# Rotary embedding: a second buffer for VectorE's sin products, so that a pass needs no separate wait instruction on VectorE

**Chip, cores, metric.** One core of one Trainium2 chip. The metric is device time in microseconds (us), the median of several runs.

## The reference

```python
batch, seq, dim, num_heads = 16, 512, 1024, 16          # x is float32, cos and sin are [seq, 32]
x = x.reshape(batch, seq, num_heads, head_dim)          # head_dim 64
x1, x2 = x[..., :half_dim], x[..., half_dim:]
rotated = np.concatenate([x1 * cos - x2 * sin,
                          x1 * sin + x2 * cos], axis=-1)
```

33.55 MB are read and 33.55 MB written. Per element there are some three arithmetic operations.

## The kernel before

x is cut into 8 slabs of 128 partitions x 8192 elements (4 MB each). Five slabs fit at a time; each is loaded by SyncE's queue and stored from the same memory by ScalarE's queue. A slab is worked on in two passes of 128x4096. In each pass ScalarE casts to bf16, VectorE makes a sin product (`t2`), a cos product in place and an add in place, and ScalarE converts back to f32.

```python
slabs  = ctx.enter_context(tc.tile_pool(name="slabs", bufs=slots))     # slots = 5
tpool  = ctx.enter_context(tc.tile_pool(name="tpool", bufs=3))         # xb, bf16
t2pool = ctx.enter_context(tc.tile_pool(name="t2pool", bufs=1))        # the sin products
# ... loads, tables ...
for i, u in enumerate(passes):
    if i + 1 < len(passes):
        cast(passes[i + 1])                       # ScalarE: xb <- slab
    s, k = u
    xs, xu = slab[s], xb.pop(u)
    t2 = t2pool.tile([P, PW], bf16, tag="t2")
    for t, a in ((t2, rpp * hd), (xu, 0)):        # sin product, then cos product in place
        nc.vector.tensor_mul(
            out=t, in0=xu,
            in1=view(tab, a + k * rows * hd, (hd, rows), (0, nh), (1, hd)))
    nc.vector.tensor_add(
        out=xu, in0=xu,
        in1=view(t2, half, (hd, rows * nh), (-half, 2), (1, half)))
    nc.scalar.copy(out=view(xs, k * PW, (1, PW)), in_=xu)              # back to f32
    if k == rpp // rows - 1:
        nc.scalar.dma_start(out=dram(out_flat, s), in_=xs)             # store
        if s + slots < nslabs:
            load(s + slots)
```

A framework orders the instructions of each engine and puts in the waits. With one `t2` buffer, the sin product of a pass must wait for the add of the pass before (which reads `t2`) as well as for ScalarE's cast. An instruction here carries one wait; the second becomes an instruction of its own ahead of it.

## Time and profile before

| | before |
|---|---|
| time, median of 3 | 162.83 us (162.74 to 163.21) |
| span of the profiled run | 160.8 us |
| VectorE busy, ScalarE busy | 111.7 us (69%), 114.8 us (71%) |
| moved by DMA | 67.25 MB, 418 GB/s over the span |

In the table of instruction groups a line gives the source line, the engine and operation, output and input, the count; then busy time and mean ns of one; then the idle time of the engine just ahead of them and what ended it. These are ScalarE's two conversions and VectorE's sin product, before:

```profile
L117 ACT CAST xb<-slab 128x4096 bf16<-128x4096 f32 x16 | 57.5, 3601 | 24.8 <-DMA slab<-in_x_dram 24.8
L137 ACT CAST slab<-xb 128x4096 f32<-128x4096 bf16 x16 | 57.7, 3604 | 7.2 <-DVE xb L133 7.1
L130 DVE TENSOR_TENSOR t<-xb,tab 128x4096 bf16<-128x4096 bf16 x16 | 36.7, 2292 | 19.4 <-ACT xb L117 18.6
```

Read from the last line upwards: VectorE's idle time is ended by ScalarE, and most of ScalarE's by DMA. The separate wait instructions stand in the view of VectorE's source line, as entries of its queue (minimum, median and maximum ns, then first and last start):

```profile
L130 DVEq EVENT_SEMAPHORE  x16: 21/21/21, 13.3 to 136.8; - x16
```

### The profile page before, as it was taken

To read this page: it belongs to the slowest core of one execution; us is meant where nothing else is said; L and a number is where in the kernel's file an instruction comes from. 1 tells how busy PE (TensorE), PEld (TensorE's weight loads), DVE (VectorE), ACT (ScalarE), POOL (GpSimd) and SP (SyncE) were. 2 spreads that over 40 slices of the span, in tenths; PEclk is the share of its full clock that TensorE was granted. 3 is DMA by queue.
4 is the path that set the end of the run, shared out by engine and by line. 5 is a ranking of instruction groups with operands and counts; after the bars stand their busy time and mean duration, and the time that the engine had idled before them with its cause. 6 is when DMAs were issued, how large, how long until landed. Compare 5 with 4: busy or idle time off the path is not lost.

```text
span 160.8 us, 197 instructions
## 1 busy us (share of the span) xinstructions
PE 0.6 (0%) x4; PEld 0.4 (0%) x4; DVE 111.7 (69%) x52; ACT 114.8 (71%) x33; POOL 2.3 (1%) x9
## 2 busy tenths in 40 slices
PE   0010000000000000000000000000000000000000
PEld 0000000000000000000000000000000000000000
DVE  0012799999999999999997599907997079970000
ACT  3007919999999999999994999069990699926000
POOL 5000000000000000000000000000000000000000
DMA  7999999999999999999999999999999999999993
GB/s 261 408 408 416 497 391 391 505 408 367 416 391 473 440 391 456 457 391 424 489 391 424 489 391 399 514 391 391 522 391 393 489 416 399 481 424 399 481 424 139
DMA packets 2369, 67.25 MB, mean 418 GB/s; under 512 B 288, under 2 KB 288, under 8 KB 320
## 3 DMA queue, kind: packets, MB, share of 16 engines
q1 hardware_dynamic: 1152, 33.55, 49.3%
q10 hardware_dynamic: 1152, 33.55, 48.3%
q0 software_dynamic: 64, 0.13, 0.2%
q14 instruction: 1, 0.01, 0.0%
HBM read 33.69 MB, written 33.55 MB: 418 GB/s over the span
## 4 chain that ended last, share of the span: by engine, by line
DMA 47%; ACT 22%; DVE 21%; issue 0%; ACTq 0%; SPq 0%; DVEq 0%
DMA slab<-in_x_dram 26%; DMA out_dram<-slab 21%; ACT slab L137 11%; ACT xb L117 11%; DVE xb L133 7%; DVE t L130 7%; DVE xb L130 7%; ACTq L137 0%; SPq L65 0%; DVEq L130 0%
## 5 line engine op out<-in xcount | busy, mean ns | idle before, releaser
L117 ACT CAST xb<-slab 128x4096 bf16<-128x4096 f32 x16 | 57.5, 3601 | 24.8 <-DMA slab<-in_x_dram 24.8
L137 ACT CAST slab<-xb 128x4096 f32<-128x4096 bf16 x16 | 57.7, 3604 | 7.2 <-DVE xb L133 7.1
L130 DVE TENSOR_TENSOR t<-xb,tab 128x4096 bf16<-128x4096 bf16 x16 | 36.7, 2292 | 19.4 <-ACT xb L117 18.6
L133 DVE TENSOR_TENSOR xb<-xb,t 128x4096 bf16<-128x4096 bf16 x16 | 36.7, 2292 | 0.5
L130 DVE TENSOR_TENSOR xb<-xb,tab 128x4096 bf16<-128x4096 bf16 x16 | 36.7, 2292 | 0.5
L92 DVE CAST tab<-raw 128x256 bf16<-128x256 f32 x1 | 0.3, 295 | 10.9 <-DMA raw<-in_sin_dram 10.9
L117 ACT ACT_TABLE_LOAD x1 | 1.3, 1283 | 0.7 <-PEq L158 0.7
L102 DVE CAST tab<-acc 128x512 bf16<-128x512 f32 x1 | 0.7, 692 | 0.7 <-PE acc L96 0.7
L75 POOL DMA_DIRECT2D raw<-in_cos_dram x1 | 0.7, 674 | 0.8 <-POOLq L158 0.8
L96 PE MATMUL acc<-tab,pick 128*128 128x128 bf16 x4 | 0.6, 302 | 11.2 <-DVE tab L92 11.2
L87 POOL TENSOR_SCALAR_AFFINE_SELECT pick<-pick 128x128 bf16<-128x128 bf16 x2 | 0.5, 288 | 0.1
L75 POOL DMA_DIRECT2D raw<-in_sin_dram x1 | 0.5, 534 | 0.0
L96 PEld LDWEIGHTS <-pick 128*128 128x128 bf16 x4 | 0.4, 128 | 11.1 <-issue 8.0
L104 DVE CAST tab<-acc 128x256 bf16<-128x256 f32 x1 | 0.4, 414 | 0.0
L106 DVE TENSOR_SCALAR tab<-acc 128x256 bf16<-128x256 f32 x1 | 0.4, 412 | 0.0
L84 POOL MEMSET pick<- 128x256 bf16 x1 | 0.3, 330 | 0.0
L158 POOL MEMSET const-float32-0.0<- 128x1 f32 x1 | 0.1, 99 | 0.2 <-issue 0.2
L158 POOL MEMSET const-uint8-127<- 128x1 uint8 x1 | 0.1, 102 | 0.0
L158 POOL MEMSET const-bfloat16-1.0<- 128x1 bf16 x1 | 0.1, 101 | 0.0
L158 POOL MEMSET const-float32-1.0<- 128x1 f32 x1 | 0.1, 98 | 0.0
## 6 DMA issues: line engine op xcount, KB each, us to landing
slab<-in_x_dram SPq DMA_DIRECT2D x8, 4096.0 KB, 28.2
out_dram<-slab ACTq DMA_DIRECT2D x8, 4096.0 KB, 28.4
raw<-in_cos_dram POOLq DMA_DIRECT2D x1, 64.0 KB, 6.9
raw<-in_sin_dram POOLq DMA_DIRECT2D x1, 64.0 KB, 8.9
```

The source lines that it names most:

```text
L75: nc.gpsimd.dma_start(out=view(raw, i * TR * half, (1, TR * half)), in_=bass.AP(tensor=src.tensor, offset=src.offset, ap=[[TR * half, P], ...
L84: nc.gpsimd.memset(pick, 0.0)
L87: nc.gpsimd.affine_select(out=part, in_=part, compare_op=mybir.AluOpType.not_equal, fill=1.0, base=-g, pattern=[[0, P // SP], [-G, SP]], c ...
L96: nc.tensor.matmul(view(acc, i * TW + g * TR * half, (1, TR * half)), view(pick, g * P, (1, P)), view(tab1, i * TR * half, (1, TR * half)) ...
L102: nc.vector.tensor_copy(out=view(tab, 0, (hd, 2 * rpp), (1, half)), in_=view(acc, 0, (half, 2 * rpp), (1, half)))
L104: nc.vector.tensor_copy(out=view(tab, half, (hd, rpp), (1, half)), in_=view(acc, 0, (half, rpp), (1, half)))
L106: nc.vector.tensor_scalar_mul(out=view(tab, rpp * hd + half, (hd, rpp), (1, half)), in0=view(acc, TW, (half, rpp), (1, half)), scalar1=-1.0)
L117: nc.scalar.copy(out=xb[u], in_=view(slab[s], k * PW, (1, PW)))
L130: nc.vector.tensor_mul(out=t, in0=xu, in1=view(tab, a + k * rows * hd, (hd, rows), (0, nh), (1, hd)))
L133: nc.vector.tensor_add(out=xu, in0=xu, in1=view(t2, half, (hd, rows * nh), (-half, 2), (1, half)))
L137: nc.scalar.copy(out=view(xs, k * PW, (1, PW)), in_=xu)
L158: nc = _bacc.Bacc("TRN2", target_bir_lowering=False, num_devices=1)
```

## The change

It is meant to let the sin product of a pass begin without asking whether the previous add has ended, so that VectorE has one wait, in the instruction itself, and no instruction for the other.

```diff
-    t2pool = ctx.enter_context(tc.tile_pool(name="t2pool", bufs=1))
+    t2pool = ctx.enter_context(tc.tile_pool(name="t2pool", bufs=2))
```

## The prediction

> **What bounds the kernel now.** I read four views: busy shares of the engines, the table by stage, the groups with what ended their idle time, then the tail in order of time. The page comes first.
>
> ```profile
> PE 0.6 (0%) x4; PEld 0.4 (0%) x4; DVE 111.7 (69%) x52; ACT 114.8 (71%) x33; POOL 2.3 (1%) x9
> DVE  0012799999999999999997599907997079970000
> ACT  3007919999999999999994999069990699926000
> DMA  7999999999999999999999999999999999999993
> DMA 47%; ACT 22%; DVE 21%; issue 0%; ACTq 0%; SPq 0%; DVEq 0%
> ```
>
> No compute engine is busy over 71% of the span, and both ScalarE and VectorE show holes late in it. The row that has none is DMA: 9 in every slice but the first and the last. The chain of waits gives VectorE 21%, which looks like room for a gain; the table by stage says why that is not to be believed. Its columns are: stretch, its length, PE, PEld, DVE, ACT, POOL busy, clock, DMA share, GB/s.
>
> ```profile
> 13.20:34.60 21.40, 0.00 (x0) 0.00 (x0) 17.27 (x9) 17.79 (x6) 0.00 (x0) 1.00 1.02 439
> 34.60:62.97 28.37, 0.00 (x0) 0.00 (x0) 27.60 (x13) 28.32 (x9) 0.00 (x0) 1.00 0.97 408
> 62.97:97.50 34.53, 0.00 (x0) 0.00 (x0) 30.97 (x15) 31.98 (x10) 0.00 (x0) 1.00 1.02 440
> 97.50:126.10 28.60, 0.00 (x0) 0.00 (x0) 20.44 (x9) 17.57 (x5) 0.00 (x0) 1.00 1.00 433
> 126.10:147.50 21.40, 0.00 (x0) 0.00 (x0) 13.75 (x6) 17.82 (x5) 0.00 (x0) 1.00 0.99 426
> 147.50:158.20 10.70, 0.00 (x0) 0.00 (x0) 0.00 (x0) 0.00 (x0) 0.00 (x0) 1.00 1.01 438
> ```
>
> Stage length times DMA share, summed, is 21.8 + 27.5 + 35.2 + 28.6 + 21.2 + 10.8 = 145.1 us of the 145.0 us from 13.2 to 158.2: the 16 DMA engines never lack work, whatever VectorE and ScalarE do (27.60 us of VectorE in one stage, 13.75 in another). The time is thus the 67.25 MB that the page counts (418 GB/s over the span), the start and the last store's completion.
>
> **What the Trainium skill says, and whether the trace agrees.** "Perfetto Trace Analysis", Identifying Dependency Chains: an instruction that waits on more than one engine may get an EventSemaphore instruction ahead of it for the further condition. The trace agrees: VectorE's queue holds 16 EVENT_SEMAPHORE of 21 ns, one ahead of each sin product, which waits both for ScalarE's cast of its input and for VectorE's own last read of the only sin buffer. "VectorE: DVE Perf Modes", The DRAIN you can't avoid: the next operation does not start before the pipe is empty, and a semaphore after each operation cost nothing extra in its measurement. The trace agrees for a wait inside an instruction (starts 2.32 to 2.33 us apart for operations of 2.29 us), and differs a little for the separate instruction, as shown below. "DMA: Bandwidth & Descriptors", Issuing engines are not separate DMA queues: loads and stores from different engines run on the same 16 DMA engines and interleave. Here loads take 49.3% and stores 48.3% of 16 engines' span, together 97.6%. The same page, Specifications, states a ceiling of 435 GB/s; the stages run at 408 to 440, so there is no faster DMA rate to be set free.
>
> **The change part by part.** It removes the second wait from 15 of the 16 sin products: the built program keeps it only on the first (which waits for the tables); the other 15 wait for ScalarE alone. No operation, shape or byte changes. It also moves something, which the diff does not show and the order of the built program does: the sin product of the second pass goes ahead of the first pass's add, and so ScalarE does three casts before its first conversion back, where it did two. From the third pass on the order is as before.
>
> What one wait costs, from the timeline of VectorE (start, duration):
>
> ```profile
> 19.21 2.29 DVE L130 TENSOR_TENSOR xb<-xb,tab 128x4096 bf16<-128x4096 bf16 x1
> 21.54 2.29 DVE L133 TENSOR_TENSOR xb<-xb,t 128x4096 bf16<-128x4096 bf16 x1
> 23.93 2.29 DVE L130 TENSOR_TENSOR t<-xb,tab 128x4096 bf16<-128x4096 bf16 x1
> 26.26 2.29 DVE L130 TENSOR_TENSOR xb<-xb,tab 128x4096 bf16<-128x4096 bf16 x1
> ```
>
> From the cos product to the add it is 21.54 - 19.21 = 2.33 us, from the add to the next sin product 23.93 - 21.54 = 2.39 us. So the separate wait costs some 0.06 us, and all 15 at most 0.9 us of VectorE, 0.6% of the span, were VectorE the bound. It isn't: in the groups the sin products' idle time is 19.4 us, 18.6 of it ended by ScalarE's cast, over 8 waits; at those the wait instruction is passed while the data are still missing. That leaves about 7 x 0.06 = 0.4 us of VectorE, and in the full stretch ScalarE is as tight: a cast and a conversion start 3.51 to 3.59 us after one another, some 7.05 us a pass, against 3 x 2.33 = 6.98 us of VectorE. VectorE will mostly wait a little longer for ScalarE.
>
> What the moved order costs: I step through it with the durations above. First sin and cos products as before, to 21.5; second sin product 21.54 to 23.84 (its cast ended at 20.36); first add 23.86 to 26.16, which is 2.33 us later than before; second cos product to 28.49; second add to 30.8, as before. ScalarE's third cast needs the second load, which was issued at about 1.3 us and took 21.8, so it runs from 23.1 to 26.7; first conversion back to 30.25, some 2.7 us later than before; second from 30.85 to 34.45 (before: 30.96 to 34.57). So the first store is issued at about 34.5 instead of 34.60 us, and the third sin product starts at 30.83 instead of 31.07. The delay is absorbed before anything outside the chip's memory notices; stores then come 0.1 to 0.4 us earlier through the full stretch. On a DMA that is busy without a break, an earlier store only takes its turn from a load.
>
> The tail is the one place where VectorE seems to be on the path:
>
> ```profile
> 126.13 3.62 ACT xb L117
> 134.42 2.30 DVE xb L133
> 136.72 0.03 issue
> 136.75 0.02 DVEq L130
> 136.77 0.04 issue
> 136.82 2.30 DVE t L130
> 143.85 3.60 ACT slab L137
> ```
>
> From the add's end at 136.72 to the sin product's start at 136.82 it is 0.10 us; with no separate wait I expect 0.03, hence the last store is issued 0.06 us earlier than 147.49. But the store before it was issued at 133.27 and took 17.0 us to land, to 150.3, so the last store stands behind it for nearly 3 us of landing time less the completion. The sum: 0 to -0.1 us of the span, and the rest of it hidden.
>
> **The rivals.** First, VectorE is the bound and its waits add up: the chain's 21% and full VectorE slices between 30 and 80 us speak for it, the unbroken DMA row and 15 x 0.06 against it. It would give at most 0.9 us, 161.9 us. Second, the moved order delays the start: the first conversion is 2.7 us later, and if the first store were late by as much and the DMA ran dry, it would cost up to 2.7 us, 165.5. Against it: five loads are issued in the first 3.2 us and the fifth takes 64.5 us to land, so the queue is full at 34.5 us, and the second conversion, not the first, releases the store. Third, the changed times mix loads and stores otherwise and the DMA rate changes: the stages lie between 408 and 440 GB/s. A change of 0.3% in the mean would be 0.5 us, either way; nothing in the profile says which. Fourth, the larger pool moves other buffers to addresses that VectorE or DMA serve otherwise. The operations last 2291 to 2294 ns in all three input buffers, which speaks against it; it would make 0.
>
> **Range and chances.** Base 162.83 us, less 0 to 0.1: I predict 162.8. The runs of before spread from 162.74 to 163.21, and the third rival may add 0.5 us to either side, so the range is 162.2 to 163.5. Two per cent would be 3.3 us: a gain of that size is over three times all the waits together (1%), a loss of that size is beyond the second rival's worst (2%); within 2% has 97%.
>
> **What would show it.** Right: the 16 EVENT_SEMAPHORE of VectorE's queue are 1 or 2; a sin product that ScalarE doesn't delay starts 2.33 us after the add ahead of it; the sin product's idle time stays near 19 us or grows; the first conversion starts at about 26.7 and the first store at about 34.5; DMA row unbroken, span 160.3 to 161.3. Wrong: gaps in the DMA row before the last slice, the first store later than 36 us, an operation whose duration changes, or a time that falls by more than 0.9 us, which would mean that VectorE's waits set the pace through the DMA in a way I don't see.

## The result, and the profile after

The changed kernel took 162.53 us (median of 6 runs, 162.28 to 162.89), the kernel before 162.74 us (6 runs, 162.29 to 163.21). The ratio is 0.9993, with a 95% interval of 0.997 to 1.0015: the same. (A ratio is the mean time of one kernel's fast runs over that of the other's of the same rounds, so not quite the ratio of the medians.) The profiled run has a span of 160.8 us, as before.

The page's busy shares after (tenths of 40 equal slices):

```profile
DVE  0003799999999999999997599907997099950000
ACT  3006939899999999999984999069990899744000
DMA  6999999999999999999999999999999999999993
```

The table by stage, in the same stretches as in the prediction:

```profile
34.60:62.97 28.37, 0.00 (x0) 0.00 (x0) 27.37 (x13) 28.26 (x9) 0.00 (x0) 1.00 1.00 415
...
97.50:126.10 28.60, 0.00 (x0) 0.00 (x0) 20.45 (x9) 18.33 (x6) 0.00 (x0) 1.00 1.01 435
126.10:147.50 21.40, 0.00 (x0) 0.00 (x0) 13.75 (x6) 17.11 (x5) 0.00 (x0) 1.00 1.00 430
```

The DMA share is 1.00 or 1.01 in every stage (the two left out too), the row has no gap, and the holes of VectorE and ScalarE are where they were.

The separate waits are gone but for the first, and VectorE's idle time ahead of the sin products is nearly what it was (18.8 against 19.4 us), ended by ScalarE as before:

```profile
L130 DVEq EVENT_SEMAPHORE  x1: 21/21/21, 13.5 to 13.5; - x1
```

```profile
L130 DVE TENSOR_TENSOR t<-xb,tab 128x4096 bf16<-128x4096 bf16 x16 | 36.7, 2291 | 18.8 <-ACT xb L117 18.4
```

The timeline after (start, duration), with the moved order at the start:

```profile
19.46 2.29 DVE L130 TENSOR_TENSOR xb<-xb,tab 128x4096 bf16<-128x4096 bf16 x1
21.67 2.28 DVE L130 TENSOR_TENSOR t<-xb,tab 128x4096 bf16<-128x4096 bf16 x1
...
26.73 3.60 ACT L137 CAST slab<-xb 128x4096 f32<-128x4096 bf16 x1
28.39 2.29 DVE L133 TENSOR_TENSOR xb<-xb,t 128x4096 bf16<-128x4096 bf16 x1
30.61 2.29 DVE L130 TENSOR_TENSOR t<-xb,tab 128x4096 bf16<-128x4096 bf16 x1
...
34.41 0.38 ACTq L139 DMA_DIRECT2D out_dram<-slab  x1
...
37.92 2.29 DVE L130 TENSOR_TENSOR t<-xb,tab 128x4096 bf16<-128x4096 bf16 x1 [0.38 <-ACT xb L117]
```

The first conversion (26.73) and the first store (34.41) came as the prediction stepped them out (26.7 and 34.5). But two starts do not fit it: the second sin product begins 21.67 - 19.46 = 2.21 us after the operation ahead of it, the third 30.61 - 28.39 = 2.22 us after the add, where 2.33 was expected. Such an operation begins before the one ahead has ended (19.46 + 2.29 = 21.75). Thereafter each sin product begins 0.03 to 0.04 us after ScalarE's cast of its input has ended, as at 37.92. Before the change it was 0.03 to 0.07 us, from the third sin product on. So all that the removed wait gives there is at most 0.04 us a pass.

In the tail the last store was issued at 146.70 us instead of 147.49, 0.79 us earlier, mostly because the last load landed at 125.36 instead of 126.11. Yet the span did not shrink. The transfer's time to landing took it back; the last number in each line, first before and then after:

```profile
out_dram<-slab ACTq DMA_DIRECT2D x1, 4096.0 KB, 12.4
```

```profile
out_dram<-slab ACTq DMA_DIRECT2D x1, 4096.0 KB, 13.2
```

147.49 + 12.4 and 146.70 + 13.2 are both 159.9. The store ahead of it landed at 150.3 in both (133.27 + 17.0; 132.52 + 17.8), 9.6 us before the last.

### The profile page after: what moved, and what is told of

It is laid out like the page before. It is cut to its first block, busy times and chain, and to the rows that moved or that the text cites. A ratio compares the mean times of both kernels' runs of the same rounds, so it can differ in the third digit from the quotient of the medians.

```text
span 160.8 us, 182 instructions
## 1 busy us (share of the span) xinstructions
PE 0.6 (0%) x4; PEld 0.4 (0%) x4; DVE 111.3 (69%) x52; ACT 114.8 (71%) x33; POOL 2.3 (1%) x9
## 2 busy tenths in 40 slices
DMA packets 2368, 67.24 MB, mean 418 GB/s; under 512 B 288, under 2 KB 288, under 8 KB 320
## 4 chain that ended last, share of the span: by engine, by line
DMA 47%; ACT 25%; DVE 13%; issue 6%; ACTq 0%; SPq 0%
DMA slab<-in_x_dram 25%; DMA out_dram<-slab 22%; ACT slab L137 16%; ACT xb L117 9%; DVE xb L133 4%; DVE t L130 4%; DVE xb L130 4%; ACTq L137 0%; SPq L65 0%
## 5 line engine op out<-in xcount | busy, mean ns | idle before, releaser
L130 DVE TENSOR_TENSOR t<-xb,tab 128x4096 bf16<-128x4096 bf16 x16 | 36.7, 2291 | 18.8 <-ACT xb L117 18.4
L133 DVE TENSOR_TENSOR xb<-xb,t 128x4096 bf16<-128x4096 bf16 x16 | 36.7, 2292 | 0.5
L130 DVE TENSOR_TENSOR xb<-xb,tab 128x4096 bf16<-128x4096 bf16 x16 | 36.7, 2292 | 0.5
L92 DVE CAST tab<-raw 128x256 bf16<-128x256 f32 x1 | 0.3, 294 | 11.1 <-DMA raw<-in_sin_dram 11.1
```

What stands on the lines that cost most here:

```text
L130: nc.vector.tensor_mul(out=t, in0=xu, in1=view(tab, a + k * rows * hd, (hd, rows), (0, nh), (1, hd)))
L133: nc.vector.tensor_add(out=xu, in0=xu, in1=view(t2, half, (hd, rows * nh), (-half, 2), (1, half)))
```

## The experiments

The theory: the 16 DMA engines have work without a break, so what VectorE saves is waited out elsewhere. The rivals: VectorE's waits count after all; the moved order gains or costs what the waits cost or gain. A second question is the size of a wait, 0.06 us or more.

### No compute at all

```diff
-    cast(passes[0])
-    for i, u in enumerate(passes): ...          # casts, products, adds, conversions
+    for s in range(nslabs):
+        nc.scalar.dma_start(out=dram(out_flat, s), in_=slab[s])
+        if s + slots < nslabs:
+            load(s + slots)
```

> Every slab is stored as it was loaded: the same 67 MB in the same 16 large transfers, no cast, product or add (the result is wrong on purpose). DMA theory: 159 to 163 us, within 2% of before, although 112 us of VectorE and 115 us of ScalarE are gone. Rival (VectorE and ScalarE are on the path, as the chain's 21% and 22% say): clearly under 155 us, since the last store no longer waits 21.4 us after the last load.

161.79 us (161.76 to 161.87), wrong result; ratio to before 0.9939, interval 0.9917 to 0.9962. Its page (67.24 MB moved, 420 GB/s):

```profile
DMA  7999999999999999999999999999999999999994
```

With the casts, products and adds of every pass gone, 0.9 us of the medians went, 0.6%. The stores also go out earlier (the first at 13.36 us instead of 34.60), so loads and stores mix otherwise; the 0.9 us is what both gave together. It is the measured room for a change on VectorE and ScalarE with these transfers. The rival's 155 us is out.

### VectorE slower by 11 us

```diff
+    junk = singles.tile([P, 2 * rpp * hd], bf16, tag="junk")
     ...
+        nc.vector.tensor_mul(out=junk, in0=view(xu, 0, (1, 2 * rpp * hd)), in1=tab)
         nc.vector.tensor_add(
```

> One more VectorE product of 128x1024 in each pass, some 0.7 us, 11 us in all, right result. VectorE becomes slower than ScalarE in a pass (7.7 against 7.05 us). DMA theory: the full stretch grows but DMA stays fed; only the two passes behind the last load reach the last store, so it comes some 1.4 us later, of which the 1 us of margin takes a part: 163 to 165 us. Rival (VectorE bound): +11 us, 173 to 175 us.

164.15 us (163.96 to 164.35), correct; ratio 1.0088, interval 1.0061 to 1.0115. The added group:

```profile
L134 DVE TENSOR_TENSOR junk<-xb,tab 128x1024 bf16<-128x1024 bf16 x16 | 11.1, 692 | 0.5
```

11.1 us more of VectorE cost 1.5 us of time. The last store was issued at 150.21 us, 2.7 us later than before (I had expected 1.4: the last load landed about 1.3 us later too), and the span grew by only 1.4 (162.2 against 160.8). The store ahead of it landed 1.3 us later than before (134.54 + 17.0 = 151.5), and the last one 9.8 us behind that (150.21 + 11.1 = 161.3). So what was paid came with the later load; the slower passes after it stayed hidden behind the store ahead, where I had expected them to cost. The run is not quite clean: the scheduler also put two casts ahead of the second conversion, so that the first store went out at 38.9 us.

### The moved order alone, the removed waits alone

```diff
 order alone (one sin buffer; 13 of the 15 removed waits are back):
+    own = singles.tile([P, PW], bf16, tag="own")
-        t2 = t2pool.tile([P, PW], bf16, tag="t2")
+        t2 = own if i == 1 else t2pool.tile([P, PW], bf16, tag="t2")

 waits alone (two sin buffers): the second pass's sin product is ordered behind the first add,
 by an order that needs no wait
+            if i == 1 and t is t2:
+                tc.add_manual_dep(m.ins, last.ins.name, mybir.DependencyInfo(
+                    mybir.DependencyClass.NoSync, mybir.DependencyReason.DATA), reason="order")
```

> One sin buffer as before, but the second pass's sin product has a tile of its own: the moved order of the change with 13 of its 15 removed waits put back. DMA theory: same as before within 0.3%, first store at about 34.4 us. Rival (the moved order is what gains or costs, the waits do the opposite): a difference of over 0.5 us to before.

> Two sin buffers as in the change, but the second pass's sin product is kept behind the first pass's add: the removed waits without the moved order. DMA theory: same as before within 0.3%, first conversion back at 23.9 us again, one separate wait instruction left on VectorE's queue. Rival (each removed wait counts): 0.9 us less by the prediction's 0.06 us each, 2.5 us less by the 0.17 us that the trace after the change suggests.

Order alone: 162.68 us (162.52 to 162.79), ratio 0.9992, interval 0.9973 to 1.0011. Waits alone: 162.36 us (162.23 to 162.86), ratio 0.9977, interval 0.9957 to 0.9998. Both are correct, and the traces show that each edit did its part. VectorE's separate waits with order alone (waits alone has one left, as the changed kernel has):

```profile
L131 DVEq EVENT_SEMAPHORE  x14: 21/21/21, 13.3 to 136.0; - x14
```

In waits alone the first conversion started at 24.84 us, not at the expected 23.9; its first cast began 0.9 us later than in before too (14.16 against 13.25), since the first load landed later. Its first store went out at 35.48 us, 0.9 us later than before, and nothing was lost by it. Neither part moves the time by the rival's amounts (0.9 or 2.5 us). But the interval of waits alone lies just under 1, so it and the changed kernel were run again, on one chip and in the same rounds:

> The changed kernel once more, on the same chip and in the same rounds as waits_again. DMA theory: a ratio to before between 0.997 and 1.003, whose interval holds 1. Rival (the interval of waits_only, 0.9957 to 0.9998, was a real gain of the removed waits): a ratio near 0.998 again, here and in waits_again, with the whole interval under 1.

> The kernel of waits_only once more. DMA theory: the 0.0023 under 1 was scatter from chip to chip and run to run, and the ratio moves towards 1. Rival: it stays near 0.998.

The changed kernel: 162.58 us, ratio 0.9987 (0.9967 to 1.0007). Waits alone: 162.58 us, ratio 0.9989 (0.9968 to 1.001). Both intervals hold 1, as the theory said. A gain of the order of 0.1% can neither be shown nor ruled out by these runs.

### DMA taken away: does VectorE come to the surface?

Only two slabs are loaded and only the last is stored; the passes use the two in turn (wrong result; only one slab of the output is written).

```diff
     def load(s):
+        if s >= 2:
+            slab[s] = slab[s % 2]
+            return
     ...
-            nc.scalar.dma_start(out=dram(out_flat, s), in_=xs)
+            if s == nslabs - 1:
+                nc.scalar.dma_start(out=dram(out_flat, s), in_=xs)
```

> Only two slabs are loaded and one is stored; the passes use the two slabs in turn (wrong result on purpose), one sin buffer, order of before. DMA no longer sets the pace after 23 us, ScalarE should: 16 passes of 7.05 to 7.1 us behind the first load, then a store of 12.4 us, together some 146 us. Layer theory: the waits are hidden a second time, behind ScalarE.

> As nodma_one with two sin buffers. Layer theory (ScalarE bounds what DMA doesn't): 0 to 0.4 us less than nodma_one. Rival (VectorE would be the bound once DMA is gone): 0.9 to 2.6 us less.

Both took 147.9 us (one buffer 147.85 to 148.01, two 147.8 to 147.9). The spans are 145.9 and 145.5 us: the 146 of the expectation was the span's size, to which the time adds some 2 us. Still no gain from the second buffer, and the timeline says why; first one buffer, then two:

```profile
80.67 3.61 ACT L140 CAST slab<-xb 128x4096 f32<-128x4096 bf16 x1
...
94.85 3.60 ACT L140 CAST slab<-xb 128x4096 f32<-128x4096 bf16 x1
```

```profile
80.20 3.60 ACT L140 CAST slab<-xb 128x4096 f32<-128x4096 bf16 x1
80.33 2.29 DVE L133 TENSOR_TENSOR t<-xb,tab 128x4096 bf16<-128x4096 bf16 x1 [0.22 <-ACT xb L120]
...
83.71 3.60 ACT L120 CAST xb<-slab 128x4096 bf16<-128x4096 f32 x1
...
87.34 2.29 DVE L133 TENSOR_TENSOR t<-xb,tab 128x4096 bf16<-128x4096 bf16 x1
...
94.38 3.60 ACT L140 CAST slab<-xb 128x4096 f32<-128x4096 bf16 x1
```

Two passes take 14.18 us in both (94.85 - 80.67; 94.38 - 80.20). With two buffers VectorE is ready sooner and waits 0.22 us for ScalarE's cast. The 14.18 us are one round through both engines: 3.51 us from a conversion to the next cast, 3.63 from that cast to its sin product, 4.66 from there to the add, 2.38 from the add to its conversion (80.20, 83.71, 87.34, 92.00, 94.38; with one buffer 80.67, 84.18, 87.81, 92.47, 94.85, the same steps). The sin product in it waits for its cast, so the removed wait isn't on the round. Four of ScalarE's conversions and casts back to back, at 3.51 us each, would take some 14.04 us (an estimate), so ScalarE alone isn't quite the pace. This round is the second layer over the wait, and the real kernels run at the same pace while their slabs are loaded in advance: their second and third stores are issued 14.18 us apart, before (48.79, 62.97) and after (48.59, 62.77).

### ScalarE thinned out too: the wait by itself

On top of the edit above, ScalarE casts only a quarter of each pass after the first three, and converts back only a quarter of every pass (wrong result). With two buffers the order on VectorE is held as it is with one.

```diff
+    xfix = [singles.tile([P, PW], bf16, tag=f"xfix{n}", name=f"xfix{n}") for n in range(3)]
-        xb[u] = tpool.tile([P, PW], bf16, tag="xb", name="xb")
-        nc.scalar.copy(out=xb[u], in_=view(slab[s], k * PW, (1, PW)))
+        n = PW if c < 3 else PW // 4              # c counts the casts
+        xb[u] = xfix[c % 3]
+        nc.scalar.copy(out=view(xb[u], 0, (1, n)), in_=view(slab[s], k * PW, (1, n)))
...
-        nc.scalar.copy(out=view(xs, k * PW, (1, PW)), in_=xu)
+        nc.scalar.copy(out=view(xs, k * PW, (1, PW // 4)), in_=view(xu, 0, (1, PW // 4)))
```

> As nodma_one, and ScalarE casts and converts back only a quarter of each pass after the first three (wrong result on purpose), so that VectorE alone sets the pace: one sin buffer. A pass should take 2.33 + 2.33 + 2.39 = 7.05 us, 16 passes about 113 us, whole program some 141 us.

> As vec_one with two sin buffers and the same order on VectorE. The disputed size: by the prediction's 0.06 us a wait, 15 x 0.06 = 0.9 us less than vec_one; by the trace after the change, in which a sin product that waits neither for ScalarE nor for the add starts 2.22 us after the add, 15 x 0.17 = 2.5 us less.

One buffer: 144.65 us (144.6 to 144.72). Two buffers: 141.94 us (141.88 to 141.99). The totals are higher than I had summed (141 for one buffer), but the difference is what was asked for: 2.71 us, or 2.71 / 15 = 0.18 us a wait. The timelines show it directly, one buffer first:

```profile
64.05 2.29 DVE L141 TENSOR_TENSOR xfix<-xfix,t 128x4096 bf16<-128x4096 bf16 x1
66.44 2.29 DVE L138 TENSOR_TENSOR t<-xfix,tab 128x4096 bf16<-128x4096 bf16 x1
```

```profile
62.82 2.29 DVE L145 TENSOR_TENSOR xfix<-xfix,t 128x4096 bf16<-128x4096 bf16 x1
65.03 2.29 DVE L138 TENSOR_TENSOR t<-xfix,tab 128x4096 bf16<-128x4096 bf16 x1
```

From add to sin product it is 2.39 us with the wait and 2.21 us without. The second buffer thus does for VectorE three times what I had predicted, and in the real kernel nothing of it is to be seen.

### What in the wait costs: the instruction or the waiting?

The last edit undone in one point: the scheduler may order VectorE as it likes with two buffers. It mixes two passes (sin, sin, cos, cos, add, add), so that nearly every operation stands behind one that it has nothing to do with; 13 sin products get their separate wait instruction back.

> As vec_two, but the order on VectorE is left to the scheduler, which mixes two passes: nearly every operation now stands behind one of the other pass and waits for nothing that has only just ended; 12 of the sin products have their separate wait instruction back. If the cost lies in waiting for the operation just ahead (0.11 us: 2.33 against 2.22 us from start to start), and a separate wait instruction costs nothing by itself: some 44 operations by 0.11 us less than vec_one for the mixed order, 138 to 140 us. If the cost lies in the separate instruction (0.06 us each, 12 of them back): no faster than vec_two, 142 us or more.

138.08 us (137.9 to 138.35), 6.57 us less than with one buffer and in order (it ran on another chip, on which before took 162.62 instead of 162.88 us). The timeline (the view merges two like operations, x2):

```profile
66.07 4.49 DVE L141 TENSOR_TENSOR xfix<-xfix,t 128x4096 bf16<-128x4096 bf16 x2
70.48 4.49 DVE L138 TENSOR_TENSOR t<-xfix,tab 128x4096 bf16<-128x4096 bf16 x2
74.88 4.49 DVE L138 TENSOR_TENSOR xfix<-xfix,tab 128x4096 bf16<-128x4096 bf16 x2
```

Two operations take 4.40 to 4.41 us, 2.20 each, sin products with a separate wait included. So no cost of the wait instruction is to be seen when what it waits for ended an operation or more ago. What costs is to wait for the operation just ahead: 0.12 us where the wait is in the instruction (2.33 against 2.21), 0.18 where it has an instruction of its own (2.39 against 2.21). The working in the expectation (44 x 0.11 = 4.8 us) left out the further 0.06 us of the 15 separate waits, and took 0.11 for what is 0.12 to 0.13; a pass fell from 7.05 to 3 x 2.20 = 6.61 us, and 15 x 0.44 = 6.6.

## Why the prediction was right, and where it wasn't

- **The bound.** Right. The DMA engines are the bound, and taking away the compute of all passes bought 0.6% (the run without compute). One reading was loose: the stage at 440 GB/s has a DMA share of 1.02, more than the whole; at a share of 1.00 it would be 440 / 1.02 = 431 GB/s.
- **The second layer.** Right that VectorE is held by ScalarE, but not by ScalarE alone at "some 7.05 us a pass": the round of cast, three VectorE operations and conversion takes 7.09 us a pass (14.18 / 2), and the real kernels run at that pace early on.
- **The moved order.** Right in its steps: first conversion 26.73 (26.7 predicted), first store 34.41 (34.5). Its rival, a late first store, did not come about, and order alone ran at 0.9992.
- **The size of one wait.** Wrong. The step that failed is "So the separate wait costs some 0.06 us, and all 15 at most 0.9 us of VectorE". It compared a separate wait with a wait in the instruction, as if the change left the latter in place; but after the change the sin product doesn't wait for the add at all. The term is 0.18 us a wait and 2.7 us for 15, as measured with DMA and ScalarE out of the way. The rival's worst case should have been 160.1 us, not 161.9. The forecast did not suffer because almost nothing of this term reaches the total: it is hidden behind ScalarE's casts, and then behind DMA. For the same reason the sign "starts 2.33 us after the add" proved wrong (2.22). Nor could "The trace agrees for a wait inside an instruction" be read from the products and adds before: each of them waits for the one just ahead, so none shows what such a wait costs. Elsewhere that trace did show a start without such a wait, where VectorE converts the tables (128x256, another shape and source):

```profile
12.47 0.41 DVE L104 CAST tab<-acc 128x256 bf16<-128x256 f32 x1
12.80 0.41 DVE L106 TENSOR_SCALAR tab<-acc 128x256 bf16<-128x256 f32 x1
```

The second begins 0.08 us before the first has ended (12.47 + 0.41 = 12.88), as the unwaited sin products did after the change. An estimate of 2.29 - 0.08 = 2.21 us from start to start could have been made from here.

- **The tail.** The last store was to come 0.06 us earlier; it came 0.79 us earlier. 0.75 us of this is the last load, which landed earlier. The other 0.04 us is the removed wait: the last sin product begins 2.36 us after the add ahead of it instead of 2.40, and no sooner because it then waits for ScalarE's cast. Why the load came earlier is not settled: the cast behind it began at 125.42 us with order alone and at 125.56 with waits alone, against 126.13 before, so no part of the change can be named for it. The changed kernel itself had it at 125.38 and, in the repeat, at 125.80, so two traces of one kernel differ by over half as much. The step that mattered held, and all seven traces of kernels with the right result show it: the last store landed 9.6 to 9.8 us after the one ahead of it, whether it was issued 1.3 us before that one landed (VectorE slower) or 3.6 us (the changed kernel). So issuing it earlier gains nothing. What was predicted, 0 to 0.1 us of gain, is not contradicted, and not shown.
- **The third rival**, another mix of loads and stores, stayed within the scatter of the runs. **The fourth**, other addresses, isn't seen: the three groups of VectorE last 2291 to 2292 ns on average, before and after.

## What to carry to other kernels

Before you buy time on an engine, take away the engine's work altogether and see how much time goes: here all the passes' work on VectorE and ScalarE was worth 0.9 us, which leaves no more for a better buffer. Then see whether the wait to be removed lies on the round that sets the pace: here, after the change, each sin product from the fourth on begins as ScalarE's cast of its input ends. A share in the chain of waits (VectorE 21%, after the change 13%, at the same time) is no measure of that. Where VectorE does set the pace, one of these 128x4096 bf16 operations loses 0.12 us when it waits for the one just ahead, or 0.18 with a separate wait instruction, and mixing two independent passes wins it back: 7.05 to 6.61 us a pass of three 2.29 us operations.

## What the Trainium skill lacked or had wrong

- "VectorE: DVE Perf Modes", The DRAIN you can't avoid, says that chaining operations without semaphores can't skip the flush, and that in its measurement, of tensor_copy, the semaphore cost nothing extra. For these 128x4096 bf16 products and adds a wait on the operation just ahead does cost: 2.33 us from start to start with it, 2.20 to 2.21 without. The same section also says that an operation that is not held starts earlier. That agrees with these traces, but it gives no time for it; here such a start lies some 0.08 us before the end of the one ahead.
- "Perfetto Trace Analysis", Identifying Dependency Chains, says that a separate EventSemaphore may be inserted for waits on several engines, but gives no cost: here 0.06 us beyond a wait inside the instruction when it waits for the operation just ahead, and none to be seen when that ended an operation or more ago (2.20 us from start to start with it).
- No page that I read says that a single-buffered scratch tile makes such a second wait appear, and that a second buffer also lets the scheduler reorder: one changed number removed 15 wait instructions and moved a sin product ahead of an add.
